# A weight tile's cast at each end of attention, tied behind the casts of a head's transposes

## The chip, the core and the metric

The program runs on one NeuronCore of a Trainium2 chip. The metric is the device time of one execution in microseconds (us); for the kernel before it is 1846.85 us, the median of three runs. Five engines have queues of their own: TensorE (PE), VectorE (DVE), ScalarE (ACT), GpSimd (POOL) and SyncE (SP). An engine takes the instructions of its queue in the order in which the program was built, and an instruction whose input isn't there yet holds what stands behind it.

## The reference, cut to what matters

The model has two layers, a Fourier branch and then an attention branch, on 256 tokens and 256 context tokens of width 2048. The change lies in the second layer alone: 64 query heads of width 64 in 8 groups that share keys and values, each of 256 queries against 512 keys with a sink, then a gate and the output projection.

```python
def _attend_with_sink(q, k, v, sink, mask=None):
    s = jnp.einsum('bqhgd,bkhd->bhgqk', q, k).astype(jnp.float32) * (ATTN_HEAD_DIM ** -0.5)
    if mask is not None:
        s = jnp.where(mask, s, NEG_INF)
    sk = jnp.broadcast_to(sink.astype(jnp.float32)[None, :, :, None, None], s.shape[:-1] + (1,))
    p = jax.nn.softmax(jnp.concatenate([s, sk], axis=-1), axis=-1)[..., :-1]
    return jnp.einsum('bhgqk,bkhd->bqhgd', p.astype(v.dtype), v)
...
    y = jnp.moveaxis(o, 0, 1).reshape(b, n, D_BRANCH) * jax.nn.silu(z)
...
        x = x + gate * (y @ w_out[i])
```

## The kernel before

Every float32 product is made of three fast ones. An operand is split into a high part, which is its rounding to the fast format, and a low part, which is what the rounding lost. `split` does it: a cast on ACT (line 62) and a subtraction on DVE (line 63), and it keeps the two instructions in `last_cast` and `last_sub`. A weight tile `raw` of 128 x 2048 comes by a DMA on SP's queue (three buffers); `half_split` makes `wh` and `wl` of 1024 columns from one of its halves (six buffers, so three pairs). `mm3` (lines 75 to 77) multiplies: high by high, high by low, low by high.

Attention runs two streams through each other. The first is a list of units, `ulist`: for each group of heads eight `q` units (the query projection, 12 matmuls of 512 columns each; `finish_q` then applies the rope), the `z` units (the gate; lines 1052 and 1054), and at the end twelve `o` units (the first part of the output projection, `o1_step`, with weights from `w1_next`). `emit_unit` emits the next unit and, ahead of it, the weight halves of the unit after (`prep`). The first ten units are emitted before the loop over heads begins. `filler` calls `emit_unit`.

The second stream is the heads, in a pipeline of three steps:

- `stage_s(i)`: the scores (lines 1088 and 1089, two query blocks), mask and row maximum on DVE (1090), two exponentials on ACT (1093), the sink's `es` (1094), sum and reciprocal on DVE (1095, 1096), and the scaling of the two blocks of `p` on ACT (1098).
- `stage_t`: eight transposes of `p` on PE (1108) and two splits into `ph` and `pl` (lines 62 and 63 again).
- `stage_o(i)`: eight matmuls of 256 columns, probabilities by values (1122 with `ph`, 1123 with `pl`), a copy `ot` (1128) and an add (1129).

The loop that weaves them, with the line numbers of the profile:

```python
1148            for i in range(66):
...
1152                if i < 64:
1153                    pts[i] = stage_s(i)
1154                if i >= 2:
1155                    stage_o(i - 2, ptt.pop(i - 2))
1156                filler()
1157                if 1 <= i < 65:
1158                    ptt[i - 1] = stage_t(pts.pop(i - 1))
1159                filler()
```

After the loop the rest of the `o` units' kind runs outside the list: `for k in range(12, NB, 2): w = w1_next()` and two `o1_step` each; before its first use it also splits the last gated values (`act` and `ys` in the order of time). Two larger parts of the output projection follow, and then the norm.

The text order is not the order on the engines. A scheduler takes the whole program when it is built and puts each engine's instructions in an order of its own, by priority and by the times that it expects; `tc.issue_after(ins)` makes the instructions inside its block that run on the engine of `ins` stand behind `ins` in that engine's queue.

Of the kernel before, what the change touches and what calls it, by code (L numbers as in the profile page):

```python
# [28 lines left out]
def tile_dit(ctx: ExitStack, tc: tile.TileContext, a: dict, out: bass.AP):  # L29
# [13 lines left out]
    def raw(src, q=None):  # L43
        t = rawp.tile([P, D], F32, tag="raw", name="raw")
        n = src.shape[-1]
        last_dma[0] = (q or nc.sync).dma_start(t[:, :n], src).ins
        return t
# [11 lines left out]
    last_cast, last_sub = [None], [None]  # L59
# [5 lines left out]
    def half_split(t, i):  # L65
        h = wsp.tile([P, 1024], F32R, tag="ws", name="wh")
        l = wsp.tile([P, 1024], F32R, tag="ws", name="wl")
        split(h, l, t[:, i * 1024 : (i + 1) * 1024])
        return h, l

    def ws_split(t):
        return [half_split(t, i) for i in range(2)]
# [71 lines left out]
    def split_part(nm, t):  # L144
        l = wfp.tile([P, 8, 127], F32R, tag="wf", name=f"w{nm}l")
        h = wfp.tile([P, 8, 127], F32R, tag="wf", name=f"w{nm}h")
        split(h, l, t)
        return h, l

    def split_uh(v, m):  # L150
        return {"m": split_part("m", m), "p": split_part("p", v)}
# [364 lines left out]
    for g in range(G):  # L516
        if g == 2:
            mix0 = ft_end[0]
        if g == 3:
            with tc.issue_after(f0_end[0]):  # L520
                f3 = [fold_uh(load_uh(g, kh), g, kh) for kh in range(2)]
            w = [split_uh(*f3[0]), {"m": split_part("m", f3[1][1])}]
# [3 lines left out]
        elif g == 4:  # L526
            w = []
# [6 lines left out]
        elif g > 4:  # L534
            with tc.issue_after(evacs[g - 2][1]):
                f3 = [fold_uh(load_uh(g, kh), g, kh) for kh in range(2)]
            w = [split_uh(*f3[0]), {"m": split_part("m", f3[1][1])}]
            v = f3[1][0]
        else:
            w = wu[g]  # L540
# [117 lines left out]
    with tc.tile_pool(name="yp", reuse_waits="tile", bufs=32) as ypool:  # L658
# [20 lines left out]
        with tc.tile_pool(name="zp", reuse_waits="tile", bufs=2) as zp:  # L679
# [11 lines left out]
            for kg in range(4):  # L691
                wr = raw(a["wz0"][kg])
                w = []
# [5 lines left out]
                for j in range(4):  # L699
                    k = kg * 4 + j  # L700
# [9 lines left out]
            for b in range(4, NB):  # L710
                w = ws_split(raw(a["wz"][b - 4]))
# [44 lines left out]
        for i in range(32):  # L756
# [3 lines left out]
            w = ws_split(raw(a["wo0"][sw, kg]))  # L760
# [85 lines left out]
    with tc.tile_pool(name="h1", reuse_waits="tile", bufs=16) as h1p:  # L846
# [3 lines left out]
        with tc.tile_pool(name="kvp", reuse_waits="tile", bufs=2) as kvp:  # L850
# [20 lines left out]
            for kg in range(8):  # L871
                with tc.issue_after(h_end[0]), tc.issue_after(sq_end[0]):
                    w = ws_split(raw(a["wkv"][kg])) if kg else [w0, half_split(wr, 1)]
                for j in range(2):
                    k = kg * 2 + j
# [33 lines left out]
        with tc.tile_pool(name="at", reuse_waits="tile", bufs=2) as at:  # L909
# [4 lines left out]
            def w1_next():  # L914
                n = kg1[0]
                kg1[0] += 1
                if n % 2 == 0:
                    raw1[0] = raw(a["wo1a"][n // 2])
                return half_split(raw1[0], n % 2)
# [9 lines left out]
            def o1_step(k, os_, wh, wl):  # L929
                while len(yh) <= min(k + 4, NB - 1) and (len(yh) < 24 or fin):  # L930
                    y_split(len(yh))
                for tb in range(2):
                    mm3(os_[tb], yh[k][:, tb * P : (tb + 1) * P], yh[k][:, N + tb * P : N + (tb + 1) * P], wh, wl, k == 0, k == NB - 1)
# [141 lines left out]
            def stage_s(i):  # L1075
                hk, blk, hh = i // 8, i // 2, i % 2
                p2, pr = (blk % 4) // 2, blk % 2
                kkh, kkl = kk[hk]
                q2 = qq[hk, p2][hh]
                pt = at.tile([P, 2, 512], F32, tag="p", name="p")  # L1080
                mx = at.tile([P, 2], F32, tag="mx", name="mx")
                sm = at.tile([P, 2], F32, tag="sm", name="sm")
                es = at.tile([P, 2], F32, tag="es", name="es")
                so = []
                for tb in range(2):
                    o = psum()
                    st = q2[:, (pr * 2 + tb) * P : (pr * 2 + tb + 1) * P]
                    PE.matmul(o, st, kkh, start=True, stop=False)  # L1088
                    PE.matmul(o, st, kkl, start=False, stop=True)  # L1089
                    V.tensor_tensor_reduce(o, o, mask[:, tb, :], -0.125, nsink[:, i : i + 1], ALU.add, ALU.min, mx[:, tb : tb + 1])  # L1090
                    so.append(o)
                for tb in range(2):
                    S.activation(pt[:, tb, :], so[tb], AF.Exp, bias=mx[:, tb : tb + 1], scale=-1.0, accum_out=sm[:, tb : tb + 1])  # L1093
                S.activation(es, mx, AF.Exp, bias=sink[:, i : i + 1])
                V.tensor_tensor(sm, sm, es, op=ALU.add)
                V.reciprocal(sm, sm)  # L1096
                for tb in range(2):
                    S.activation(pt[:, tb, :], pt[:, tb, :], AF.Copy, scale=sm[:, tb : tb + 1])  # L1098
                return pt

            def stage_t(pt):
                res = []
                for kp in range(2):
                    o = psum()
                    for kt in range(2):
                        for tb in range(2):
                            c = (kp * 2 + kt) * P
                            PE.transpose(o[:, (kt * 2 + tb) * P : (kt * 2 + tb + 1) * P], pt[:, tb, c : c + P], ident)  # L1108
                    ph = at.tile([P, 512], F32R, tag="ph", name="ph")
                    pl = at.tile([P, 512], F32R, tag="pl", name="pl")  # L1110
                    split(ph, pl, o)
                    res.append((ph, pl))
                return res

            def stage_o(i, pts):
                hk, blk, hh = i // 8, i // 2, i % 2
                oo = psum()
                for kb in range(4):
                    ph, pl = pts[kb // 2]
                    q = slice((kb % 2) * N, (kb % 2 + 1) * N)  # L1120
                    st = v2[kb][hk // 4][:, (hk % 4) * P : (hk % 4 + 1) * P]
                    PE.matmul(oo[:, 0:N], st, ph[:, q], start=kb == 0, stop=False)  # L1122
                    PE.matmul(oo[:, 0:N], st, pl[:, q], start=False, stop=kb == 3)  # L1123
                if hh == 0:
                    obs[blk, 0] = at.tile([P, N], F32, tag="ob", name="ob", bufs=4)
                ob = obs[blk, 0]
                t = at.tile([64, N], F32, tag="ot", name="ot", bufs=1)
                S.copy(t, oo[64:128, 0:N])
                V.tensor_tensor(ob[hh * 64 : hh * 64 + 64, :], oo[0:64, 0:N], t, op=ALU.add)
                if hh == 1:  # L1130
                    obs[blk, 1] = ob
                    emit_y(blk)
# [7 lines left out]
            def filler():  # L1140
                j = slot[0]
                slot[0] += 1
                emit_unit()
                if defer and defer[0][0] + 2 < j:
                    defer.pop(0)[1]()

            pts, ptt = {}, {}
            for i in range(66):
                if i % 8 == 0:
                    while defer:  # L1150
                        defer.pop(0)[1]()
                if i < 64:
                    pts[i] = stage_s(i)
                if i >= 2:
                    stage_o(i - 2, ptt.pop(i - 2))
                filler()
                if 1 <= i < 65:
                    ptt[i - 1] = stage_t(pts.pop(i - 1))
                filler()


        with tc.tile_pool(name="fin", reuse_waits="tile", bufs=1) as fp:
# [23 lines left out]
                    GP.tensor_tensor(x, x, fg[:, q], op=ALU.mult)  # L1186

            for k in range(12, NB, 2):
                w = w1_next()
                for i in range(2):  # L1190
                    o1_step(k + i, oA, *(t[:, i * 512 : (i + 1) * 512] for t in w))
            for tb in range(2):
# [2 lines left out]
            for kg in range(16):  # L1195
                w = ws_split(raw(a["wo1b"][kg]))
                for j in range(2):
                    k = kg * 2 + j
# [37 lines left out]
            for kg in range(8):  # L1236
                t = raw(a["wo1c"][kg])
                if kg < 5:
                    w = [(h[:, q], l[:, q]) for h, l in ws_split(t) for q in (slice(0, 512), slice(512, 1024))]
                else:  # L1240
                    w = []
# [129 lines left out]
```

## Time and profile before

| | |
|---|---|
| three runs | 1846.19, 1846.85, 1848.97 us |
| profiled execution: own time | 1846.4 us |
| profiled execution: span | 1844.5 us |
| granted clock of PE over the span | 0.998 |

The span goes from the first to the last instruction of the profiled execution. The lines of the profile name the kernel's line, the engine, the operation, output and input tiles and the shape; in the order of time the first two numbers are the start and the duration in us, and a bracket gives the idle time of the engine ahead of the instruction and what ended it. PE's matmuls overlap: one of 512 columns is listed with 0.39 us, while the next starts earlier than that.

### The profile page before, as it was taken

Reading aid. Unit: us, or ns where it says so; the run is one execution under the profiler, and the core shown is the slowest. Engines: PE = TensorE matmul, PEld = TensorE weight load, DVE = VectorE, ACT = ScalarE, POOL = GpSimd, SP = SyncE. Lnnn points to the kernel's source line nnn. Section 1 sums busy time; section 2 is a strip of 40 time slices with the busy share of each in tenths; the row PEclk is TensorE's granted clock in tenths of the full one; section 3 lists DMA queues with packets and bytes.
Section 4 is the critical chain, followed back from the end, with each engine's and each line's share of the span. In section 5 each row is a group of like instructions: output and inputs, shape, how many; then the busy total and the mean of one; then the engine's idle time right before and its main releaser. Section 6 shows DMA issues by size and latency. Waiting matters only on the chain.

```text
span 1844.5 us, 26534 instructions
## 1 busy us (share of the span) xinstructions
PE 1812.6 (98%) x9917; PEld 1548.5 (84%) x9917; DVE 1395.3 (76%) x2777; ACT 958.1 (52%) x1662; POOL 173.8 (9%) x185
## 2 busy tenths in 40 slices
PE   6999999999999999999999999999999999999997
PEld 5689999888888888888888888888888888888886
DVE  5688888787878887858874836878878878887455
ACT  5444444432222242214222625888888888897343
POOL 0001212000000000000000001121220220300001
PEclk9999999999999999999999999999999999999999
DMA  9988889666666648553575324333333333444553
GB/s 394 417 314 233 222 232 275 225 226 224 243 244 262 235 169 294 214 214 114 206 286 208 115 95 156 123 130 138 115 117 135 135 117 137 160 138 179 186 182 137
DMA packets 74593, 366.37 MB, mean 199 GB/s; under 512 B 21153, under 2 KB 21809, under 8 KB 39393
## 3 DMA queue, kind: packets, MB, share of 16 engines
q1 hardware_dynamic: 50400, 326.67, 48.2%
q0 software_dynamic: 19920, 31.06, 6.6%
q10 hardware_dynamic: 4144, 6.95, 1.2%
q8 instruction: 78, 1.28, 0.3%
q14 instruction: 51, 0.41, 0.1%
HBM read 352.06 MB, written 12.59 MB: 198 GB/s over the span
## 4 chain that ended last, share of the span: by engine, by line
PE 93%; DMA 3%; DVE 2%; ACT 1%; issue 1%; POOL 0%; POOLq 0%; SPq 0%; ACTq 0%; DVEq 0%
PE ps L75 24%; PE ps L76 24%; PE ps L77 24%; PE ps L1052 6%; PE ps L1054 3%; PE ps L1108 3%; DMA raw<-in_awp 2%; PE ps L1123 2%; PE ps L1122 2%; PE ps L1088 2%; PE ps L1089 2%; PE ps L213 1%; DMA raw<-in_wu 1%; PE ps L968 0%; DMA xn<-in_x 0%
## 5 line engine op out<-in xcount | busy, mean ns | idle before, releaser
L62 ACT CAST wh<-raw 128x1024 fp32r<-128x1024 f32 x333 | 349.9, 1052 | 548.7 <-PE ps L76 465.1
L63 DVE TENSOR_TENSOR wl<-raw,wh 128x1024 fp32r<-128x1024 f32 x333 | 421.9, 1269 | 231.3 <-ACT wh L62 228.2
L76 PE MATMUL ps<-act,wh 128*128 128x512 f32 x1024 | 398.2, 389 | 0.0
L75 PE MATMUL ps<-act,wh 128*128 128x512 f32 x1024 | 394.5, 389 | 0.0
L77 PE MATMUL ps<-act,wl 128*128 128x512 f32 x1024 | 392.8, 389 | 0.0
L77 PEld LDWEIGHTS ps<-act,wl 128*128 128x128 f32 x1024 | 192.2, 188 | 39.9
L76 PEld LDWEIGHTS ps<-act,wh 128*128 128x128 f32 x1024 | 192.2, 188 | 39.8
L75 PEld LDWEIGHTS ps<-act,wh 128*128 128x128 f32 x1024 | 192.2, 188 | 39.8
L1052 PE MATMUL ps<-h,wh 128*128 128x512 f32 x512 | 186.4, 399 | 0.0
L645 DVE CUSTOM_DVE_ANT_0 raw<-raw,cb 128x512 f32<-128x512 f32 x256 | 172.7, 689 | 9.5 <-DMA raw<-in_adw 5.8
L645 DVE CUSTOM_DVE_ANT_0 junk<-raw,cb 128x512 f32<-128x512 f32 x192 | 132.0, 687 | 32.1 <-DMA raw<-in_adw 20.3
L1054 PE MATMUL ps<-h,wl 128*128 128x256 f32 x512 | 138.2, 280 | 0.0
L76 PE MATMUL ps<-wl,h 128*128 128x512 f32 x320 | 125.4, 392 | 0.0
L77 PE MATMUL ps<-wh,h 128*128 128x512 f32 x320 | 124.2, 391 | 0.0
L75 PE MATMUL ps<-wh,h 128*128 128x512 f32 x320 | 123.6, 396 | 0.5 <-ACT h L859 0.5
L1052 PEld LDWEIGHTS ps<-h,wh 128*128 128x128 f32 x512 | 96.0, 188 | 18.4
L1090 DVE CUSTOM_DVE_ANT_0 ps<-ps,mask,nsink 128x512 f32<-128x512 f32 x128 | 92.1, 754 | 11.7 <-PE ps L1089 10.6
L1093 ACT ACTIVATE p<-ps,mx 128x512 f32<-128x512 f32 x128 | 87.4, 687 | 24.8 <-DVE mx L1090 24.2
L1054 PEld LDWEIGHTS ps<-h,wl 128*128 128x128 f32 x512 | 96.8, 189 | 1.4
L63 DVE TENSOR_TENSOR pl<-ps,ph 128x512 fp32r<-128x512 f32 x128 | 83.7, 685 | 9.8 <-ACT ph L62 9.0
L1098 ACT ACTIVATE p<-p,sm 128x512 f32<-128x512 f32 x128 | 85.4, 716 | 7.8 <-DVE sm L1096 7.8
L75 PE MATMUL ps<-act,wph 128*127 128x260 f32 x256 | 73.5, 287 | 1.1 <-DVE act L241 1.1
(321 smaller groups left out, 3578.8 us busy)
## 6 DMA issues: line engine op xcount, KB each, us to landing
raw<-in_wz SPq DMA_DIRECT2D x64, 1024.0 KB, 4.9
raw<-in_adw SPq DMA_DIRECT2D x64, 1024.0 KB, 5.1
raw<-in_awp SPq DMA_DIRECT2D x32, 1024.0 KB, 13.0
raw<-in_wo SPq DMA_DIRECT2D x32, 1024.0 KB, 5.3
raw<-in_wq SPq DMA_DIRECT2D x32, 1024.0 KB, 4.9
raw<-in_wu SPq DMA_DIRECT2D x32, 1016.0 KB, 8.0
raw<-in_wo1b SPq DMA_DIRECT2D x16, 1024.0 KB, 4.8
act<-in_xT POOLq DMA_DIRECT2D x32, 256.0 KB, 6.2
```

What stands on the lines that cost most here:

```text
L62: last_cast[0] = S.copy(h, src).ins
L63: last_sub[0] = V.tensor_tensor(l, src, h.bitcast(F32), op=ALU.subtract).ins
L75: PE.matmul(o, wh, xh, start=start, stop=False)
L76: PE.matmul(o, wh, xl, start=False, stop=False)
L77: return PE.matmul(o, wl, xh, start=False, stop=stop).ins
L645: V.tensor_tensor_reduce(junk if s == 0 and i < 3 else wf, wf, cb[:, s, kq * 512 : kq * 512 + 512], 1.0, 0.0, ALU.mult, ALU.add, acc[:, i, ...
L1052: PE.matmul(o[0], wh[:, q], hx1[k], start=k == 0, stop=k == KT - 1)
L1054: PE.matmul(o[0][:, 0:N], wl[:, q], hx1[k][:, 0:N], start=False, stop=False)
L1090: V.tensor_tensor_reduce(o, o, mask[:, tb, :], -0.125, nsink[:, i : i + 1], ALU.add, ALU.min, mx[:, tb : tb + 1])
L1093: S.activation(pt[:, tb, :], so[tb], AF.Exp, bias=mx[:, tb : tb + 1], scale=-1.0, accum_out=sm[:, tb : tb + 1])
L1098: S.activation(pt[:, tb, :], pt[:, tb, :], AF.Copy, scale=sm[:, tb : tb + 1])
L1108: PE.transpose(o[:, (kt * 2 + tb) * P : (kt * 2 + tb + 1) * P], pt[:, tb, c : c + P], ident)
```

## The change

It ties two pieces of the weight stream to the head stream. In the loop's second step (i = 1) the second `filler` is put behind the last cast and the last subtraction of `stage_t(0)`. That filler emits unit 13 and prepares the weights of unit 14, so that the instructions of ACT and DVE in it, which are the split of unit 14's half tile, stand behind head 0's. In step 63 the last cast and subtraction of `stage_t(62)` are kept, and the first `w1_next` after the loop (k = 12), a split of one half tile, is put behind them.

```diff
                 if 1 <= i < 65:
                     ptt[i - 1] = stage_t(pts.pop(i - 1))
-                filler()
+                    t_cast, t_sub = last_cast[0], last_sub[0]
+                with tc.issue_after(t_cast) if i == 1 else nullcontext(), tc.issue_after(t_sub) if i == 1 else nullcontext():
+                    filler()
+                if i == 63:
+                    late_cast, late_sub = t_cast, t_sub
...
             for k in range(12, NB, 2):
-                w = w1_next()
+                with tc.issue_after(late_cast) if k == 12 else nullcontext(), tc.issue_after(late_sub) if k == 12 else nullcontext():
+                    w = w1_next()
                 for i in range(2):
                     o1_step(k + i, oA, *(t[:, i * 512 : (i + 1) * 512] for t in w))
```

## The prediction

> **What bounds the kernel now.** I read the page first (busy times, then the chain that ended last), then the waits of PE and a table of stretches over attention, which runs from about 1158 to 1690 us, and then the order of time at its two ends, since the diff touches nothing else.
>
> ```profile
> span 1844.5 us, 26534 instructions
> PE 1812.6 (98%) x9917; PEld 1548.5 (84%) x9917; DVE 1395.3 (76%) x2777; ACT 958.1 (52%) x1662; POOL 173.8 (9%) x185
> PE 93%; DMA 3%; DVE 2%; ACT 1%; issue 1%; POOL 0%; POOLq 0%; SPq 0%; ACTq 0%; DVEq 0%
> ```
>
> PE is busy 98% of the span and carries 93% of the chain. So a microsecond in which PE stands still inside attention is a microsecond of the kernel; the busy time of ACT and DVE counts only where PE waits for them. Where does it wait in the two stretches that the diff touches (1120 to 1230, and 1620 to 1760)?
>
> ```profile
> PE ps L1122 <- ACT ph L62: 0.7, 1, 0.7
> ```
>
> ```profile
> PE ps L1122 <- ACT ph L62: 0.4, 1, 0.4
> PE ps L1123 <- DVE pl L63: 0.3, 1, 0.3
> ```
>
> ```profile
> 1160.00:1170.00 10.00, 9.32 (x48) 7.59 (x47) 7.25 (x18) 9.91 (x21) 1.80 (x2) 1.00 0.44 139
> ...
> 1670.00:1680.00 10.00, 9.23 (x61) 7.93 (x60) 8.43 (x18) 9.08 (x21) 1.06 (x2) 1.00 0.78 296
> ```
>
> The first number after a stretch is its length, the second PE's busy time. One wait of 0.7 us at the start and two of 0.4 and 0.3 at the end are what the views show: the value product (L1122, L1123) waits for the cast `ph` or the low part `pl` of the transposed probabilities. Smaller gaps hide in PE's pace; I count them below. In total there is little to win.
>
> **What the change moves.** The scheduler's new order, compared engine by engine, differs in two places only. At the start, the high part (L62) and low part (L63) of weight tile 14 (the seventh of head group 1's eight q tiles), and with them tile 15, no longer stand ahead of the softmax of heads 0 and 1 but behind head 0's two `ph` casts; PE's 24 matmuls on these two tiles now stand behind the transposes of heads 0 and 1, and the k/q scores of head 2. At the end, the split for the output projection's k = 12 and 13, and with it that for 14 and 15, goes behind the casts of head 62; their 24 matmuls stood between the steps of heads 60 to 63 and now stand after head 62's value product. The ties add no semaphore; they fix the order in ACT's and DVE's own queues, and whatever follows the tied pair there (tile 15's pair, then the z tiles') follows later too. No instruction is added or removed. SP's queue keeps its order, so no load is passed by another; POOL swaps one add of the q rope, read some 20 us later.
>
> Rows for each step's duration (the last columns are busy time and the mean in ns of one):
>
> ```profile
> L1090 DVE CUSTOM_DVE_ANT_0 ps<-ps,mask,nsink 128x512 f32<-128x512 f32 x128 | 92.1, 754 | 11.7 <-PE ps L1089 10.6
> L1093 ACT ACTIVATE p<-ps,mx 128x512 f32<-128x512 f32 x128 | 87.4, 687 | 24.8 <-DVE mx L1090 24.2
> ```
>
> ```profile
> L63 DVE TENSOR_TENSOR wl<-raw,wh 128x1024 fp32r<-128x1024 f32 x133 | 171.9, 1293 | 40.9 <-ACT wh L62 38.1 <-PE ps L77 1.8 <-PE ps L1108 0.6
> L62 ACT CAST wh<-raw 128x1024 fp32r<-128x1024 f32 x132 | 138.6, 1050 | 30.6 <-PE ps L76 24.2 <-PE ps L1054 4.8 <-PE ps L1052 1.1
> L1098 ACT ACTIVATE p<-p,sm 128x512 f32<-128x512 f32 x128 | 85.4, 716 | 7.8 <-DVE sm L1096 7.8
> L63 DVE TENSOR_TENSOR pl<-ps,ph 128x512 fp32r<-128x512 f32 x128 | 83.7, 685 | 9.8 <-ACT ph L62 9.0
> ...
> L62 ACT CAST ph<-ps 128x512 fp32r<-128x512 f32 x128 | 69.1, 590 | 3.0 <-PE ps L1122 1.4
> ...
> L1094 ACT ACTIVATE es<-mx,sink 128x2 f32<-128x2 f32 x64 | 18.3, 286 | 0.0
> ...
> L1096 DVE RECIPROCAL sm<-sm 128x2 f32<-128x2 f32 x64 | 10.5, 165 | 1.8
> ```
>
> On ACT and DVE the next instruction of a queue starts about 0.1 us before the last one's recorded end, so a row's step in a full queue is its mean less 0.1; a waiting engine starts some 0.05 us after the end it waited for (this cast, 1168.90 + 0.59 = 1169.49, and L1122 at 1169.54 in the next section):
>
> ```profile
> 1168.90 0.59 ACT L62 CAST ph<-ps 128x512 fp32r<-128x512 f32 x1
> ```
>
> **The start.** PE's order of time before:
>
> ```profile
> 1158.28 0.39 PE L1089 MATMUL ps<-kkl,qa 128*128 128x512 f32 x1
> ...
> 1161.45 0.39 PE L75 MATMUL ps<-wh,h 128*128 128x512 f32 x1
> ...
> 1166.67 0.39 PE L77 MATMUL ps<-wh,h 128*128 128x512 f32 x1
> 1166.90 0.38 PE L1108 MATMUL ps<-ident,p 128*128 128x128 f32 x2
> ...
> 1169.54 0.39 PE L1122 MATMUL ps<-ph,act 128*128 128x256 f32 x1 [0.68 <-ACT ph L62]
> 1169.77 1.04 PE L1108 MATMUL ps<-ident,p 128*128 128x128 f32 x8
> ...
> 1171.43 0.28 PE L1122 MATMUL ps<-ph,act 128*128 128x256 f32 x1
> 1171.55 0.28 PE L1123 MATMUL ps<-pl,act 128*128 128x256 f32 x1
> ...
> 1172.75 0.39 PE L1052 MATMUL ps<-h,wh 128*128 128x512 f32 x1
> ```
>
> The first line is the second half of head 0's first score. The next two are the first and the last of the 24 moved weight matmuls: 23 steps in 5.22 us, 0.227 from start to start (512 columns), and 5.45 us in all, from 1161.45 to 1166.90. They are the cover of the softmax: in that time DVE and ACT make head 0's and head 1's probabilities. The change takes the cover away, so PE is at the transposes (L1108) at 1161.45. When are the probabilities there?
>
> ```profile
> 1157.97 1.28 ACT L1093 ACT_TABLE_LOAD   x1
> ```
>
> ```profile
> 1157.98 1.23 DVE L63 TENSOR_TENSOR wl<-raw,wh 128x1024 fp32r<-128x1024 f32 x1 [0.77 <-ACT wh L62]
> 1159.24 0.76 DVE L1090 CUSTOM_DVE_ANT_0 ps<-ps,mask,nsink 128x512 f32<-128x512 f32 x1
> ```
>
> The tied work helps here a little: the low part at 1157.98 is gone, so L1090 starts when the score ends (1158.28 + 0.39 = 1158.67), not at 1159.24, and the table load runs earlier, in ACT's idle time. From there, step by step: L1090 four times at 0.67 (1158.7 to 1161.5); head 0's two exponentials at 1159.6 and 1160.25 and its `es` at 1160.9; in ACT's new order head 1's come before head 0's scaling, so they run 1161.1 to 1162.6; head 0's scaling (L1098) 1162.6 to 1163.3. PE transposes at 1163.35: **1.9 us idle**. Two transposes, head 2's scores and six transposes bring PE to 1165.2; the four scalings keep ACT until 1165.05, the cast `ph` ends at 1165.65, and L1122 starts at 1165.7: **0.5 us idle**. Four transposes later L1123 waits for `pl` (1165.7 + 0.69): **0.15**. From there the tied casts are ready when PE comes to them. After: 2.6 us of stalls.
>
> Before, by the same count: 1166.90 to 1172.75 is 5.85 us, in which PE does 16 transposes at 0.11 (the x8 row: 1.04 less 0.27 by 7), eight score matmuls at 0.227 and nine of 256 columns at 0.12 (the L1122 and L1123 rows), 4.65 us: 1.2 us of stalls, 0.68 of them in the bracket. **Start: 2.6 - 1.2 = +1.4 us.**
>
> **The end.**
>
> ```profile
> 1666.26 0.39 PE L75 MATMUL ps<-wh,ys 128*128 128x512 f32 x1
> ...
> 1671.63 0.48 PE L1088 MATMUL ps<-kkh,qb 128*128 128x512 f32 x1
> ...
> 1679.76 0.48 PE L75 MATMUL ps<-wh,act 128*128 128x512 f32 x1
> ```
>
> At 1666.26 the first of the 24 matmuls for k = 12 to 15 begins; I call that moment 0 and walk the new order from it. Head 60's value product and head 61's transposes need 1.8 us, head 63's scores 0.9, then five of head 61's eight product matmuls: 3.3. The next needs the second `pl` of head 61. ACT's queue holds: head 62's first exponential from 0.05; the first `ph` cast at 1.1; the second exponential and `es` to 2.5; the second `ph` cast 2.5 to 3.1. DVE does head 63's two L1090 first and that `pl` from 3.9 to 4.6: **1.35 us idle**. Three matmuls on, at 5.0, PE wants head 62's probabilities: reciprocal to 4.7, `es` of head 63 in between, scaling 5.0 to 5.65 and 5.55 to 6.25: **0.7 and 0.35**. Six transposes on, at 7.0, it wants head 62's `ph`: ACT first scales head 63 (6.45 to 7.7), the cast ends at 8.25: **1.3**. Head 63's transposes and seven product matmuls end at 10.1; two weight matmuls on, the low part for k = 12 (made from 9.75 to 10.95) is late by **0.45**. Twelve W matmuls and one L1122 on, eight small splits of `act` stand ahead of the next half tile on both engines; its low part ends at 14.8: **1.0**. Sum: 5.15 us.
>
> Before, from head 63's scores (1671.63) to 1679.76, 8.13 us: 12 matmuls of 512 columns (2.7), 16 of 256 (1.9) and 16 transposes (1.8) are 6.4: 1.75 of stalls. **End: 5.15 - 1.75 = +3.4 us.** Between the ends the order is the same and PE is full, so what is lost at the start is not given back.
>
> **Sum.** +1.4 + 3.4 = +4.8 us. The profiled execution's own time is 1846.4 us (span 1844.5), which would become 1851.2; it lies 0.45 below the median of the three times shown, 1846.85. On the median: 1851.65, said as **1851.7 us**. About 0.2%, 3.7 us, is what a measurement of this kernel can tell from no change.
>
> Bounds. Every wait above could be shorter if ACT and DVE run 5% faster than their rows: the longest chains (4.6 us at the start, 8.25 at the end) shrink by 0.2 and 0.4 us, so the forecast holds from +4.0. Only if the whole loss at the end were given back would the start's +1.4 be left; if no gap that I count for before is real except the bracketed 0.68 and 0.76, it is +6.3. The loads behind the delayed tiles start later too, as their buffers come free later. I cost that at nothing: SP loads two raw tiles ahead, and PE waits for no load in either stretch.
>
> **The clock.** Can a stall slow PE beyond its length?
>
> ```profile
> 11.22 0.58 PE L75 MATMUL ps<-dh,xh 128*128 128x256 f32 x1 [11.22 <-DVE dh L181]
> ...
> 17.31 0.41 PE L75 MATMUL ps<-dh,xh 128*128 128x256 f32 x1
> ...
> 18.59 0.41 PE L75 MATMUL ps<-dh,xh 128*128 128x256 f32 x1
> ...
> 23.15 0.28 PE L75 MATMUL ps<-dh,xh 128*128 128x256 f32 x1
> ...
> 23.85 0.28 PE L75 MATMUL ps<-dh,xh 128*128 128x256 f32 x1
> ```
>
> ```profile
> 81.13 1.06 PE L213 MATMUL ps<-raw,c 128*32 128x512 f32 x8 [0.21 <-DMA raw<-in_awp]
> 83.55 1.06 PE L213 MATMUL ps<-raw,c 128*32 128x512 f32 x8 [1.35 <-DMA raw<-in_awp]
> ```
>
> After 11.2 us idle, six matmuls take 1.28 us (0.213 each) until about 19 us; later six take 0.70 (0.117). After 1.35 us idle nothing changes: eight take 1.06 as after 0.21. My longest stall, 1.9, is near the second case, so the sum has no slow stretch. The Trainium skill, "TensorE: Matmul & The Clock Gate", Part 1, says that PE falls to half its clock after an idle window of about 3.4 us; by that rule too the sum stays, unless stalls of one stretch add up.
>
> **Rivals.** *Faster: the ties do what their place suggests.* If head 0's casts and head 62's come without waiting, the stalls of before go: at most 1.2 + 1.75 = 2.95 us, 1843.9. It decides where the probabilities are ready within the PE work left ahead of them; the rows say 1163.35 against 1161.45, so against it. Chance 0.07, half of it over 0.2%.
>
> *Only one end loses.* If the runs of small waits at the end are shorter than walked, since `ph` casts come in another pace, the total stays at +1.4 to +3.7: about 1849.3. For it: six waits in series, where a later one shrinks if an earlier one grows, but the chain's length is fixed. Chance 0.13.
>
> *A clock drop.* Stalls of 3.7 us within 5 us at the end throw PE to 0.213 per 256 columns, as at the start of the kernel for 8 us: some 4 us more, 1855.7. Chance 0.04.
>
> *The change doesn't do what it says*: out, since the built order shows the moves.
>
> **How the numbers follow.** The forecast, both ends losing (+4.0 to +6.3), has 0.76; with the clock drop, slower by over 0.2% has 0.8. Within 0.2% are the one-end case and the rest of the faster one, 0.16; faster 0.04. The range reaches down to the one-end case, 1849.0, and up to +6.3 with 0.85 for the spread of the runs, 1854.0.
>
> **What would show it.** Right: PE waits at L1108 for ACT `p` L1098 by about 1.9 us near 1163 and again at the end, at L1123 for `pl`, at L1122 for `ph`, and at L76 for `wl`; the stretches 1160 to 1170 and 1665 to 1680 lose about 2.5 and 5 us of PE's busy time; the first L1052 comes some 1.4 us later than its place in the work. Wrong: no idle bracket at L1108, or PE's 512-column matmuls at more than 0.23 us after one.

## The result: slower by 7.2 us, and the profile after

The changed kernel takes 1853.59 us in the median of six runs (1851.58 to 1855.56); the kernel before, run beside it, 1846.35 (1845.64 to 1848.97). The ratio is 1.0036, with a 95% interval of 1.0026 to 1.0046, which is 4.8 to 8.5 us. The forecast was 4.85 us and 1851.7, with a range to 1854.0. The direction and most of the mechanism were right; one term was missing.

The profiled execution of the changed kernel has an own time of 1852.89 us. Its page:

```profile
span 1851.1 us, 26533 instructions
PE 1815.6 (98%) x9917; PEld 1550.4 (84%) x9917; DVE 1396.8 (75%) x2777; ACT 957.1 (52%) x1662; POOL 175.9 (10%) x185
PE 94%; DMA 2%; DVE 1%; ACT 1%; issue 0%; POOL 0%; ACTq 0%; POOLq 0%; DVEq 0%
```

Here is a first oddity. The span grew by 6.6 us and PE's busy time by 3.0, though PE has the same 9917 matmuls of the same shapes. Idle time explains only the other 3.6. Somewhere the same work took longer.

To place the loss, three moments that both kernels share: the first score matmul, the last copy of a query projection (L955, ACT's copy ahead of the rope; the last head group's queries, deep in attention) and the first add of the output projection behind attention (L1181 before, L1185 after, since the change adds four lines). Kernel before:

```profile
1158.05 0.39 PE L1088 MATMUL ps<-kkh,qa 128*128 128x512 f32 x1
1574.51 0.59 ACT L955 COPY act<-ps 128x512 f32<-128x512 f32 x1
1702.42 1.39 DVE L1181 TENSOR_TENSOR act<-ps,gbc 128x512 f32<-128x512 f32 x2
```

Changed kernel:

```profile
1157.98 0.39 PE L1088 MATMUL ps<-kkh,qa 128*128 128x512 f32 x1
1576.21 0.59 ACT L955 COPY act<-ps 128x512 f32<-128x512 f32 x1
1709.04 1.39 DVE L1185 TENSOR_TENSOR act<-ps,gbc 128x512 f32<-128x512 f32 x2
```

From the first to the second it was 416.46 us and is 418.23: the start lost **1.77 us**. From the second to the third it was 127.91 and is 132.83: the end lost **4.92 us**. Together 6.69, which is the span's growth within 0.1. These two differences are far finer than the times of whole runs (where a run below leaves one end alone, its number comes back within 0.08 us), and every experiment below is read by them.

The waits of PE in the two stretches (1120 to 1230, and 1620 to 1760), changed kernel:

```profile
PE ps L1108 <- ACT p L1098: 1.8, 1, 1.8
PE ps L1122 <- ACT ph L62: 0.3, 1, 0.3
```

```profile
PE ps L1123 <- DVE pl L63: 1.0, 1, 1.0
PE ps L1122 <- ACT ph L62: 0.9, 1, 0.9
PE ps L1108 <- ACT p L1098: 0.8, 2, 0.7
```

The predicted waits are there, but for the one at L76. In the order of time, the start:

```profile
1161.15 0.39 PE L77 MATMUL ps<-wh,h 128*128 128x512 f32 x1
1163.31 0.44 PE L1108 MATMUL ps<-ident,p 128*128 128x128 f32 x2 [1.76 <-ACT p L1098]
...
1165.67 0.39 PE L1122 MATMUL ps<-ph,act 128*128 128x256 f32 x1 [0.35 <-ACT ph L62]
```

And ACT's queue while PE waits (the first line is head 1's second exponential):

```profile
1161.69 0.68 ACT L1093 ACTIVATE p<-ps,mx 128x512 f32<-128x512 f32 x1
...
1162.35 0.29 ACT L1094 ACTIVATE es<-mx,sink 128x2 f32<-128x2 f32 x1
1162.54 2.55 ACT L1098 ACTIVATE p<-p,sm 128x512 f32<-128x512 f32 x4
```

PE is done with its weight work at 1161.4. Head 0's scaling, the first of the four at L1098, starts at 1162.54, behind the exponentials of both heads. The end:

```profile
1671.26 0.39 PE L1122 MATMUL ps<-ph,act 128*128 128x256 f32 x1
1672.64 0.39 PE L1123 MATMUL ps<-pl,act 128*128 128x256 f32 x1 [0.98 <-DVE pl L63]
...
1672.98 0.28 PE L1123 MATMUL ps<-pl,act 128*128 128x256 f32 x1
1673.92 0.44 PE L1108 MATMUL ps<-ident,p 128*128 128x128 f32 x2 [0.66 <-ACT p L1098]
1674.53 1.30 PE L1108 MATMUL ps<-ident,p 128*128 128x128 f32 x6 [0.17 <-ACT p L1098]
1676.77 0.58 PE L1122 MATMUL ps<-ph,act 128*128 128x256 f32 x1 [0.94 <-ACT ph L62]
1677.15 1.91 PE L1108 MATMUL ps<-ident,p 128*128 128x128 f32 x8
```

The last line shows what the prediction left out of its sum: eight transposes take 1.91 us, where they took 1.04 at the start of attention in the kernel before. PE runs at half speed. The stretches, cut where the clock changes (after the length: PE, weight loads, DVE, ACT and POOL busy, then the granted clock):

```profile
1671.42:1674.83 3.41, 1.59 (x9) 0.95 (x10) 1.87 (x7) 3.36 (x10) 1.05 (x2) 1.00 0.52 175
1674.83:1678.24 3.41, 2.47 (x13) 2.06 (x12) 2.19 (x5) 3.38 (x7) 0.00 (x0) 0.50 1.01 423
1678.24:1681.66 3.42, 3.42 (x15) 3.13 (x14) 3.42 (x8) 3.42 (x10) 0.00 (x0) 0.50 0.04 17
1681.66:1685.07 3.41, 3.41 (x17) 2.79 (x16) 3.41 (x7) 3.13 (x5) 0.00 (x0) 1.00 0.14 26
```

For 6.83 us the granted clock is 0.50. PE is busy 5.89 us of it (2.47 + 3.42), with work that takes half as long at full clock: 2.95 us more. This is the busy time that the page gained. In the kernel before the clock is 1.00 here.

### The profile page after: what moved, and what is told of

Same layout as the page of the kernel before. It is cut to its first block, busy times and chain, and to the rows that moved or that the text cites. A ratio compares the mean times of both kernels' runs of the same rounds, so it can differ in the third digit from the quotient of the medians.

```text
span 1851.1 us, 26533 instructions
## 1 busy us (share of the span) xinstructions
PE 1815.6 (98%) x9917; PEld 1550.4 (84%) x9917; DVE 1396.8 (75%) x2777; ACT 957.1 (52%) x1662; POOL 175.9 (10%) x185
## 3 DMA queue, kind: packets, MB, share of 16 engines
q8 instruction: 78, 1.28, 0.3%
## 4 chain that ended last, share of the span: by engine, by line
PE 94%; DMA 2%; DVE 1%; ACT 1%; issue 0%; POOL 0%; ACTq 0%; POOLq 0%; DVEq 0%
PE ps L75 24%; PE ps L76 24%; PE ps L77 24%; PE ps L1052 6%; PE ps L1054 3%; PE ps L1108 3%; DMA raw<-in_awp 2%; PE ps L1122 2%; PE ps L1123 2%; PE ps L1088 1%; PE ps L1089 1%; PE ps L213 1%; DMA dm<-in_dmat 0%; PE ps L968 0%; ACT p L1098 0%
## 5 line engine op out<-in xcount | busy, mean ns | idle before, releaser
L76 PE MATMUL ps<-act,wh 128*128 128x512 f32 x1024 | 398.2, 389 | 0.0
L76 PEld LDWEIGHTS ps<-act,wh 128*128 128x128 f32 x1024 | 192.2, 188 | 39.8
L76 PE MATMUL ps<-wl,h 128*128 128x512 f32 x320 | 125.4, 392 | 0.0
L1098 ACT ACTIVATE p<-p,sm 128x512 f32<-128x512 f32 x128 | 85.2, 716 | 8.5 <-DVE sm L1096 8.5
L76 PE MATMUL ps<-wl,ys 128*128 128x512 f32 (+1 forms) x192 | 74.7, 389 | 0.0
```

Of the source, the lines that this page charges most:

```text
L76: PE.matmul(o, wh, xl, start=False, stop=False)
```

## The experiments

Theory A is the prediction's mechanism (PE loses the cover of a softmax at each end) with the clock added: where a stretch of some 3.4 us holds too little work, PE's clock halves behind it. Theory B: the slow stretch was a state of one execution and not the waits' doing. Theory C: the two ends act on each other. The table gives the losses against the kernel before by the three moments, and the ratio of the times with its interval.

| run | start, us | end, us | ratio of times |
|---|---|---|---|
| the changed kernel | +1.77 | +4.92 | 1.0036 (1.0026 to 1.0046) |
| e1, start tie alone | +1.78 | +0.01 | 1.0006 (0.9997 to 1.0015) |
| e2, end tie alone | 0.00 | +5.28 | 1.0026 (1.0016 to 1.0035) |
| e3, end tie, stalls filled | +0.08 | +4.03 | 1.0022 (1.0013 to 1.0031) |
| e4, both ties again | +1.72 | +5.42 | 1.0033 (1.0021 to 1.0044) |
| e5, end tie behind head 60 | +0.01 | +1.31 | 1.0003 (0.9994 to 1.0012) |
| e6, start tie, head 0 unscaled | +0.40 | +0.02 | 1.0001 (0.9992 to 1.0010) |
| e7, start tie, two more copies | +6.03 | +0.03 | 1.0024 (1.0015 to 1.0033) |
| e8, start tie one head later | +5.40 | +0.03 | 1.0022 (1.0013 to 1.0032) |

### e1 and e2: one end at a time

e1 leaves out the second tie, e2 the first:

```diff
-                with tc.issue_after(late_cast) if k == 12 else nullcontext(), tc.issue_after(late_sub) if k == 12 else nullcontext():
-                    w = w1_next()
+                w = w1_next()
```

```diff
-                with tc.issue_after(t_cast) if i == 1 else nullcontext(), tc.issue_after(t_sub) if i == 1 else nullcontext():
-                    filler()
+                filler()
```

> Only the first tie: the weight split behind head 0's casts; the end is that of the kernel before. Theory A (each end loses its own uncovered softmax; PE's clock halves where a stretch of some 3.4 us holds too little work): the trace of the changed kernel lost 1.8 us between the first head's scores and the middle of attention, through waits of 1.76 us at L1108 and 0.35 at L1122, at full clock. So here +1.8 us over the kernel before (about 1848.2 against 1846.4), the same two waits, and nothing more at the end; where the 1.76 us wait falls into one stretch of the clock gate, a granted clock of 0.5 for some microseconds behind it, and up to +4. Theory B (the slow stretch at 1674 to 1681 us was a state of that one execution and has nothing to do with the waits): +1.8 with the clock at 1.00 in every stretch. Theory C (the two ends act on each other): another number than +1.8, below +1 or above +3 with the clock at 1.00.

> Only the second tie: the split for k = 12 and 13 behind head 62's casts; the start is that of the kernel before. Theory A: the four waits at L1123, L1108 (two) and L1122, 3.7 us with the idle time hidden in PE's pace, against 1.2 before, and behind them 5 to 7 us with a granted clock of 0.5: +4.9 us over the kernel before in the trace, as the changed kernel lost there (1851.3). If the gate's phase spares this run, PE instead meets waits at L76 for the low parts wl, 0.4 and 1.0 us, the clock stays at 1.00, and the loss is +3.4. Theory B (clock unrelated): +3.4 and the waits at L76 in most runs, the clock at 1.00. Theory C (the ends act on each other): a loss that together with that of the start alone does not make the loss of both within 0.5 us in the traces.

The ends are independent: 1.78 + 5.28 = 7.06, against 6.69 and 7.14 in the two traces with both ties. Theory C falls. The start's loss has the clock at 1.00 throughout. In e2 the clock halves again, at another moment and so with another loss:

```profile
1672.09:1675.50 3.41, 1.93 (x11) 1.25 (x11) 1.78 (x7) 3.39 (x10) 0.71 (x2) 1.00 0.76 267
1675.50:1682.32 6.82, 5.70 (x21) 5.24 (x22) 5.71 (x13) 6.79 (x15) 0.00 (x0) 0.50 0.43 174
```

### e3: fill the stalls with work that nothing needs

```diff
                 for kb in range(4):
...
+                    for _ in range(10 if i == 61 and kb == 0 else 0):
+                        PE.matmul(oo[:, 0:N], st, ph[:, q], start=True, stop=True)
+                    if i == 62 and kb == 0:
+                        for _ in range(9):
+                            with tc.issue_after(pe_last[0]):
+                                PE.matmul(oo[:, 0:N], st, hx1[0][:, 0:N], start=True, stop=True)
                     PE.matmul(oo[:, 0:N], st, ph[:, q], start=kb == 0, stop=False)
```

`pe_last` holds PE's last transpose or product matmul, so that the added ones stand behind it. Eight more stand in front of head 62's transposes in the same way; what they write is overwritten by the matmuls behind them. Line numbers shift: L1111 is the transpose.

> The second tie alone, as in the run with only the end, plus 27 matmuls of 256 columns whose results nothing uses, put where PE stood still: 10 ahead of head 61's value product, 8 ahead of head 62's transposes, 9 ahead of head 62's value product (each 0.12 us, 3.2 us of added PE work). Theory A: the fill takes the place of the idle time, no stretch of 3.4 us is left with over 1.3 us of idle time, the clock stays at 1.00 through the end, and the loss is about +3.9 us over the kernel before, that is 1 us less than the same kernel without the fill although PE does 3.2 us more work. Theory B: the fill can't help: at least the +4.9 of the run without it, or, if that one shows no slow clock, its loss plus 0.4.

The stretch where e2 stalled (5 us steps, e3):

```profile
1671.00:1676.00 5.00, 5.00 (x45) 4.93 (x43) 3.20 (x9) 4.88 (x12) 0.68 (x2) 1.00 0.75 315
1676.00:1681.00 5.00, 4.25 (x19) 2.94 (x18) 4.75 (x12) 5.00 (x13) 0.00 (x0) 1.00 0.25 105
1681.00:1686.00 5.00, 4.60 (x23) 3.47 (x22) 4.65 (x7) 3.47 (x6) 0.00 (x0) 1.00 0.45 162
```

```profile
PE ps L76 <- DVE wl L63: 0.8, 2, 0.4
```

27 more matmuls (3.2 us of PE's time), and the end loses 4.03 us instead of 5.28. The clock stays at 1.00, and now PE meets the waits at L76 for `wl` that the prediction had walked for an end at full clock. The granted clock of every timed execution, over the whole span, says the same: 6.83 us at half clock are 0.0018 of the span. It is 0.996 or 0.997 in all 21 executions with the end tie and no fill (changed kernel, e2, e4), and 0.998 or 0.999 in all 11 of e3. In the kernel before it is 0.998 or 0.999 in 54 of the 57 run beside the experiments, and 0.997 in three. Theory B falls: the half clock comes with the stalls, and work in their place holds the clock up.

### e4: the changed kernel again

> The changed kernel once more, on the same chip as the other three. Theory A: the stalls come again at the same places to 0.1 us (1.76 at L1108 at the start; about 1, 0.7, 0.2 and 0.9 at the end); where the granted clock is 0.5, and for how many stretches of 3.4 us, may differ, since the stretches don't start with the kernel; +5 to +9 us over the kernel before, 6.7 the middle of it, and the sum of the two single ends within 1 us. Theory B: the same stalls with the clock at 1.00 and +4.8. Theory C: as measured before, but not the sum of the two single ends.

The same stalls but one, and the clock halved again at the end (1675.70 to 1682.53), 0.9 us later than in the first trace, for a loss of 5.42 instead of 4.92. The stall that differs is the last:

```profile
PE ps L1122 <- ACT ph L62: 1.4, 1, 1.4
```

So the half clock at the end came in all three traces with this order, at three moments; its price changed with the moment. PE's busy time at half clock is nearly the same in the three (5.89 us in the first, 5.70 in e2, 6.04 here). The wait at L1122 is not: 0.9 us in the first trace, where the clock had fallen during the transposes ahead of it, and 1.4 in e2 and e4, where it fell while PE was waiting. One line of this run is kept for later, the stretch that holds the start's 1.76 us wait:

```profile
1160.29:1163.70 3.41, 1.65 (x9) 1.11 (x8) 1.47 (x8) 3.41 (x11) 0.00 (x0) 1.00 0.00 0
1163.70:1167.11 3.41, 3.06 (x23) 2.51 (x22) 2.94 (x7) 3.41 (x6) 0.00 (x0) 1.00 0.02 5
```

### e5: the end tie two heads earlier

```diff
-                if i == 63:
+                if i == 61:
                     late_cast, late_sub = t_cast, t_sub
```

(together with e2's edit at the start)

> The end tie alone, but behind head 60's casts, two heads earlier: the split for k = 12 and 13 comes ahead of the last two heads' softmax, and its 24 matmuls stand between them again. Theory A (what costs is the cover that is moved away): walked as the prediction was, three waits are left, 0.9 and 0.4 us at L1108 and 1.3 at L1122, where the kernel before has 1.2 us in all: +0.9 us over the kernel before at full clock; they lie within some 4 us, so that most of them may fall into one stretch of the clock gate, and then +2.6. Theory B (the tie itself costs, wherever it stands): the +5 of the tie behind head 62.

```profile
PE ps L1122 <- ACT ph L62: 1.4, 1, 1.4
PE ps L1108 <- ACT p L1098: 0.9, 2, 0.7
```

```profile
1671.00:1676.00 5.00, 4.19 (x23) 3.26 (x21) 4.90 (x10) 4.83 (x9) 0.00 (x0) 1.00 0.97 401
1676.00:1681.00 5.00, 3.56 (x25) 3.15 (x26) 3.67 (x11) 4.95 (x14) 0.00 (x0) 1.00 1.00 421
```

+1.31, near the walked +0.9, with the walked waits. A tie of the same pair costs 1.3 or 5 us by where it stands; what the edit changes is how many weight matmuls are left between the last heads' steps. The 2.3 us of bracketed idle time did not halve the clock in this trace.

### e6 and e7: take away and lengthen the start's wait

e6 and e7 are e1 with one edit each in `stage_s`:

```diff
-                for tb in range(2):
+                for tb in range(2 if i else 0):
                     S.activation(pt[:, tb, :], pt[:, tb, :], AF.Copy, scale=sm[:, tb : tb + 1])
```

```diff
+                for tb in (0, 1) if i == 0 else ():
+                    S.activation(pt[:, tb, :], pt[:, tb, :], AF.Copy, scale=1.0)
```

> The start tie alone, with head 0's two scalings (L1098) left out, so that head 0's probabilities are not divided by their sum. Theory A (PE waits for ACT's queue, in which head 0's scaling stands behind head 1's exponentials): head 0's probabilities are there at 1161.1, before PE wants them; the 1.76 us wait at L1108 goes, later waits of 0.6, 0.3 and 0.4 us come, and the loss falls from +1.8 to about +0.4 us. Rival (PE waits at this place for the tied weight tiles, whatever ACT does with head 0): the loss stays at +1.8.

> The start tie alone, with two more ACT passes over head 0's probabilities (multiplied by 1.0 in place, so that nothing changes in the result). Theory A (the clock gate goes by the share of idle time in a stretch of some 3.4 us): one stall at L1108 of 4.2 us instead of 1.8, so the stalls cost +4.0 us over the kernel before; over 0.6 of a gate's stretch is idle wherever the stretches begin, so the clock falls to 0.5 at about 1165 us for some 7 us, at the start now, where it stayed at 1.00 with a stall of 1.8, and the loss is +5.1 to +6.6. Theory B (the clock is not the stalls' doing, or it falls only at the end of attention): +4.0 with the clock at 1.00.

Without head 0's scaling PE has one bracketed wait left at the start:

```profile
PE ps L1123 <- DVE pl L63: 0.3, 1, 0.3
```

Three small ones had been expected. The loss falls from 1.78 to 0.40, as expected: PE waited for ACT's queue, not for the tied tiles. With two copies more (L1110 and L1100 are the transpose and the scaling):

```profile
1165.00 0.69 PE L1110 MATMUL ps<-ident,p 128*128 128x128 f32 x2 [4.12 <-ACT p L1100]
```

```profile
1160.09:1163.50 3.41, 0.79 (x4) 0.33 (x2) 1.22 (x7) 3.41 (x11) 0.00 (x0) 1.00 0.00 0
1163.50:1170.32 6.82, 5.29 (x19) 4.40 (x20) 3.01 (x7) 4.22 (x9) 0.00 (x0) 0.50 0.01 2
```

In this trace the clock halves at the start as well, for 6.82 us, and the loss is 6.03: within theory A's 5.1 to 6.6, and 2 us above the 4.0 expected for the stall alone. So e3 and e7 touch the clock from both sides: the half clock went when stalls were filled, and came where a stall was lengthened. But e7's fall is not regular, as theory A had it ("wherever the stretches begin"): the granted clock is 0.995 to 0.997 in five of its ten executions and 0.998 in the other five, as in the kernel before, where 6.83 us at half clock would have taken it to 0.997 or less. One stall of 4.1 us brought it in some executions, the several shorter ones of the end, by the same number, in all 21. Why is open.

### e8: the start tie one head later

```diff
-                with tc.issue_after(t_cast) if i == 1 else nullcontext(), tc.issue_after(t_sub) if i == 1 else nullcontext():
+                with tc.issue_after(t_cast) if i == 2 else nullcontext(), tc.issue_after(t_sub) if i == 2 else nullcontext():
                     filler()
```

(together with e1's edit)

> The start tie alone, one head later: the second filler of i = 2 behind head 1's casts. It moves the split of the first z tile. Theory A (a tie costs what it takes from PE's cover and what it holds up): the queues behind it slip past the rope of head group 1, PE meets two waits of about 2.0 and 2.8 us at the q transposes (L968) and some 2 us of smaller ones at L1122 and L1123: +6.5 us at full clock, and with the clock halved behind the two large waits +8.2 to +9.7. Theory B (a tie behind a head's casts costs what it cost at head 0, since the softmax that it uncovers is the same): +1.8.

+5.40: the price depends on the place, so this run's theory B falls, but theory A's number was too high, and its two waits at L968 did not come. What PE met instead, at 1183.37:

```profile
1183.37 0.45 PE L1054 MATMUL ps<-h,wl 128*128 128x256 f32 x1 [1.39 <-DVE wl L63]
```

The clock behind it was 0.50 for one stretch of 3.41 us:

```profile
1180.13:1183.54 3.41, 1.62 (x7) 0.88 (x6) 3.38 (x4) 3.39 (x7) 3.27 (x3) 1.00 0.00 0
1183.54:1186.95 3.41, 3.41 (x12) 2.92 (x13) 3.35 (x8) 3.38 (x8) 3.41 (x4) 0.50 0.73 250
```

Why that low part was late is told under the hardware. The walk of e8 is a miss: it had the direction, but neither the places of the waits nor the size.

## Why the prediction was right, and where it failed

**The reading of the bound.** Right. PE carried the chain before (93%) and after (94%), and what it lost inside attention came out at the end of the kernel.

**The start, +1.4.** Measured +1.77. The walk of the new order was good: 1.9, 0.5 and 0.15 us of stalls were walked. The trace has 1.93 ahead of L1108 (from 1161.38, one step behind the start of the last weight matmul, to 1163.31) and a bracket of 0.35 at L1122. The step that was mis-sized is "Before, by the same count ... 1.2 us of stalls". The new stalls, 1.93 and about 0.5 (the bracket with its hidden start), less the loss of 1.77 leave 0.7 us that really went away, about the one bracketed wait. The other 0.5 of the count are small steps in PE's pace that the changed kernel has too. e6 shows that the reason was the right one.

**The end, +3.4.** The walk's first four stalls were 1.35, 0.7, 0.35 and 1.3. By the rows above, from start to start less the pace, they are 1.26 (1671.26 + 0.12 to 1672.64), 0.82 (1672.98 + 0.12 to 1673.92), 0.39 (1673.92 + 0.22 to 1674.53), and 1.15 ahead of 1676.77 (the last transpose starts at 1675.41 and takes a step of 0.21 at half clock). The two at L76, 0.45 and 1.0, did not come in the changed kernel: PE arrived late because it ran at half speed. They came in e3, where the clock was full, as 0.4 and 0.4: the second shorter than walked.

**The clock.** This is the step that failed: "My longest stall, 1.9, is near the second case, so the sum has no slow stretch." The argument took the longest single stall, and no single stall of the changed kernel's end was longer than 1.3 us, while the longer one at its start, 1.93, left the clock at 1.00. Several stalls close together brought the half clock: 2.95 us more of PE's time, where the sum had nothing. How much idle time it takes is open (e7). The Trainium skill's "TensorE: Matmul & The Clock Gate", Part 1, was cited for an idle window of about 3.4 us, with the reserve "unless stalls of one stretch add up". They did. The trace agrees with the length that the Trainium skill gives (the half clock lasted 3.41 us or 6.83) and does not agree with a window that has to be idle: PE was busy 1.59 of the 3.41 us ahead of the fall.

**The rival with the clock drop** had the right mechanism, a chance of 0.04, and 1855.7 us, from "some 4 us more". The clock took 2.95 us, but PE's delay swallowed the two waits at L76 (1.45 us walked). What is left is 1.5, and 3.4 + 1.5 = 4.9 is the measured end. A slow PE needs its inputs later, so a clock drop among waits costs less than its own length; the wait at L1122, 0.9 us behind an early fall and 1.4 behind a late one, shows it in the rows. The same order at full clock was never seen, and the 1.45 is the walk's, so the 1.5 is worked out, not measured; e3's difference of 1.25 to e2 stands beside it, with 3.2 us of added work in it.

**The sum.** +4.8 was forecast, 6.7 us measured by the moments: 0.4 from the start's count of before and 1.5 from the clock. The other rivals are out: neither end gained, and both lose (e1, e2).

## What to carry to other kernels

A weight split that seems to stand in the way of a softmax may be what feeds the matmuls that cover it; before moving it, ask which matmuls read its result and what PE does in their place. Where the new order leaves PE several short waits within some 3 us, add them up: half clock may follow, and its price has to be counted against the waits that it hides. The granted clock of all executions tells whether one trace's half clock is the rule. For effects of a few microseconds, compare the distances between moments that both traces share; e1's 1.78 us is plain there, and not to be told from nothing in the times of eleven runs.

## What the runs showed of the hardware

**The clock fell behind stretches that were idle for about half their time or more, not at a sharp number.** Recorded busy time of PE in the 3.41 us ahead of a fall was 0.79 (e7), 1.59 (changed kernel), 1.62 (e8), 1.93 (e2) and 1.94 (e4). The 1.65 us of e4's start, quoted above, was spared, though it lies between them. Where the limit is, and whether the recorded busy time, whose ends are modelled, is the right measure, stays open. The half clock lasted 6.83 us at attention's end and in e7, and 3.41 in e8. e8's trace has another 3.41 us of it at 67 us, far ahead of the edit and of both distances; no other trace has it there.

**The moment of the fall moves from run to run.** 1674.83, 1675.50 and 1675.70 in three traces of the same end, with losses of 4.92, 5.28 and 5.42.

**DVE instructions with two inputs in SBUF were slower beside POOL.** In e8 the late low part took 2.27 us, where the mean of its row before was 1.29, while POOL made the low part of a group's keys (L944) and then began an add of the rope (L844):

```profile
1179.67 1.26 DVE L1095 TENSOR_TENSOR sm<-sm,es 128x2 f32<-128x2 f32 x1 [2.38 <-ACT es L1094]
1180.96 0.17 DVE L1096 RECIPROCAL sm<-sm 128x2 f32<-128x2 f32 x1
1181.04 2.27 DVE L63 TENSOR_TENSOR wl<-raw,wh 128x1024 fp32r<-128x1024 f32 x1
```

```profile
1179.61 2.62 POOL L944 TENSOR_TENSOR kkl<-act,kkh 64x512 fp32r<-64x512 f32 x2
1182.31 2.15 POOL L844 TENSOR_TENSOR act<-act,rt 128x512 f32<-128x512 f32 x1
```

Even a sum of two columns took 1.26 us beside POOL, and the reciprocal behind it, with one input, its usual 0.17. The two `pl` at 1184.58, which read one of their inputs from PSUM, took 1.28 together beside POOL, no more than their row before. The Trainium skill's "GPSIMD Engine Reference", section 1, says that POOL and DVE contend where a DVE instruction has two inputs in SBUF; these rows agree. No run took POOL's work away at this place, so the cause is read from the rows and not tested.
